# The opening of a four-layer decoder trunk: the input's two parts made straight from PSUM, its squares summed as loaded, and the first weights loaded in turns with the input

## The chip, the core and the metric

The kernel runs on one core of one Trainium2 chip. The metric is the device time of one execution in microseconds (us), lower is better. The core has a matrix engine (TensorE, PE in the rows; its weight loads are PEld), a vector engine (VectorE, DVE), an activation engine (ScalarE, ACT), GpSimd (POOL) and SyncE (SP), which here only issues transfers. The engines run side by side, each in the order of its own instructions, and wait for each other and for transfers at semaphores. TensorE writes only to PSUM, eight banks of 128 x 512 float32; the other tiles lie in SBUF.

## What is computed

The reference is a trunk of four layers on 256 tokens of width 1024. Each layer adds half a SwiGLU, a token mixer and another half SwiGLU to the residual stream, each behind an RMS norm:

```python
def swiglu(h, w_gate_up, w_down):
    g, u = jnp.split(h @ w_gate_up, 2, axis=-1)
    return (jax.nn.silu(g) * u) @ w_down
...
h = x
for layer in range(DEPTH):
    h = h + 0.5 * swiglu(rmsnorm(h, ffn_norm[layer, 0]), ffn_w_gate_up[layer, 0], ffn_w_down[layer, 0])
    h = h + mixer(rmsnorm(h, mixer_norm[layer]))
    h = h + 0.5 * swiglu(rmsnorm(h, ffn_norm[layer, 1]), ffn_w_gate_up[layer, 1], ffn_w_down[layer, 1])
```

The change touches only what happens before and during the first two pieces of the very first SwiGLU.

## The kernel before

All products are float32 products in three passes. Every operand is split into a high part, rounded to the matrix engine's fp32r format, and a low part, the remainder: `hi*hi + hi*lo + lo*hi`. So each weight block goes through ScalarE (`whi`, the rounded copy, `Weights.hi`, L126) and then VectorE (`wlo`, the difference, `Weights.lo`, L136). The input goes the same way: `xhi` by L294 and `xlo` by L303, both scaled by the norm's weights.

**Weights.** The class `Weights` streams all weights through four raw buffers of 128 x 2048 floats (`raw`), issued by SP in program order (L93). A raw buffer is cut into two *halves* of 128 x 1024, and each half becomes one `whi` and one `wlo`; there is room for six such halves. A *piece* of the first SwiGLU is 256 output columns (128 gate columns and 128 up columns) over all eight blocks of 128 input rows. It takes two halves: the first 128+128 columns of raw buffer 0 (input blocks 0 to 3) and those of raw buffer 1 (blocks 4 to 7). The second piece takes the other columns of the same two buffers. A piece is 8 blocks x 2 column halves x 3 passes = 48 products of 128x128 by 128x256.

**The opening.** `xin`, the input, comes in two transfers of 512 columns each (L255), then raw buffer 0 in four transfers of 128 columns (`L93`, 512-byte runs), then raw buffers 1, 2 and 3 in two transfers each with 1 KB runs. TensorE transposes `xin` into PSUM two blocks at a time (L2048, four transposes for two blocks, 16 in all), VectorE copies the result to `x` (L2050), ScalarE makes `xhi` from `x`, VectorE `xlo`, and GpSimd squares `x` (L2052). The squares are added on VectorE (L308), summed over the rows by four small products (`norm_sums`, L315), and turned into the norm's factor `rb` (`norm_rows`: L327, L329, L332), which scales the products afterwards. The products therefore need `xhi` and `xlo` but not the sum.

**Idle products.** `busy(n)` issues n products of constants (L272) that nothing reads, in places where TensorE would stand still.

**Order.** Everything is written out by hand; an engine's order is the order of the calls. The first piece is `first_cols` (blocks 0 to 3; L423 `whi` with `xhi` and `xlo` in turn, L427 `wlo`) and `late_cols` (blocks 4 to 7, L448: `whi` and `wlo` with `xhi` in turn, then `whi` with `xlo`). The second is `two_cols` (L335 to L337), with `norm_sums` before its block 2 and `norm_rows` before its block 5. Every later piece is `two_cols`; after each piece a `tail` (L486 to L502) makes the SwiGLU's hidden values from PSUM while the products of the next ones run.

## Time and profile before

| | |
|---|---|
| time of three runs | 2145.30, 2145.71, 2146.26 us; median 2145.71 |
| the profiled execution | time 2145.67 us, span 2143.9 us from the first to the last instruction |
| busy of the span | PE 99%, PEld 97%, DVE 66%, ACT 50%, POOL 13% |
| mean granted TensorE clock | 0.997 of full speed |

TensorE is busy in almost the whole span. Its busy time is the sum of modelled ends, so it is not the same as running at its peak; but a stretch in which it is not busy, or in which its clock is at half, is time that nothing later gives back as long as it is busy all the time behind it. The time that is not part of the span (1.8 us) lies around it.

### The profile page before, as it was taken

Reading aid. Unit: us, or ns where it says so; the run is one execution under the profiler, and the core shown is the slowest. Engines: PE = TensorE matmul, PEld = TensorE weight load, DVE = VectorE, ACT = ScalarE, POOL = GpSimd, SP = SyncE. Lnnn points to the kernel's source line nnn. Section 1 sums busy time; section 2 is a strip of 40 time slices with the busy share of each in tenths; the row PEclk is TensorE's granted clock in tenths of the full one; section 3 lists DMA queues with packets and bytes.
Section 4 is the critical chain, followed back from the end, with each engine's and each line's share of the span. In section 5 each row is a group of like instructions: output and inputs, shape, how many; then the busy total and the mean of one; then the engine's idle time right before and its main releaser. Section 6 shows DMA issues by size and latency. Waiting matters only on the chain. (4 is left out here: it accounts for less than half of the span.)

```text
span 2143.9 us, 42323 instructions
## 1 busy us (share of the span) xinstructions
PE 2120.5 (99%) x17599; PEld 2078.6 (97%) x17599; DVE 1408.4 (66%) x2326; ACT 1065.7 (50%) x1800; POOL 283.8 (13%) x312
## 2 busy tenths in 40 slices
PE   8999999999999999999999998999999999999999
PEld 8999999999999999999999987899999999999999
DVE  7664897665566476664666468866556648986653
ACT  5453754544454355444455445654445536655442
POOL 2210101121022010210121010012002101011110
PEclk9999999999999999999999999999999999999999
DMA  8564451556465555655566453155546563524652
GB/s 245 183 243 138 140 180 40 179 177 213 155 201 192 183 170 184 196 184 192 165 200 230 148 163 118 57 181 191 188 152 200 197 235 97 160 85 139 196 198 78
DMA packets 264304, 363.25 MB, mean 169 GB/s; under 512 B 17856, under 2 KB 212544, under 8 KB 264112
## 3 DMA queue, kind: packets, MB, share of 16 engines
q1 hardware_dynamic: 258320, 357.63, 50.8%
q8 instruction: 138, 2.26, 0.4%
q10 hardware_dynamic: 4848, 1.59, 0.4%
q0 software_dynamic: 944, 1.33, 0.3%
q14 instruction: 54, 0.44, 0.1%
HBM read 357.89 MB, written 2.10 MB: 168 GB/s over the span
## 5 line engine op out<-in xcount | busy, mean ns | idle before, releaser
L136 DVE TENSOR_TENSOR wlo<-raw,whi 128x1024 fp32r<-128x1024 f32 x640 | 775.2, 1219 | 234.8 <-ACT whi L126 234.4
L335 PE MATMUL acc<-xhi,whi 128*128 128x256 f32 x3248 | 911.4, 281 | 0.0
L337 PE MATMUL acc<-xhi,wlo 128*128 128x256 f32 x3248 | 909.4, 280 | 0.0
L336 PE MATMUL acc<-xlo,whi 128*128 128x256 f32 x3248 | 907.6, 279 | 0.0
L126 ACT ACTIVATE whi<-raw 128x1024 fp32r<-128x1024 f32 x633 | 660.2, 1050 | 352.5 <-PE mid L336 230.3
L336 PEld LDWEIGHTS acc<-xlo,whi 128*128 128x128 f32 x3248 | 611.1, 188 | 0.5
L337 PEld LDWEIGHTS acc<-xhi,wlo 128*128 128x128 f32 x3248 | 609.6, 188 | 0.0
L335 PEld LDWEIGHTS acc<-xhi,whi 128*128 128x128 f32 x3248 | 608.7, 187 | 0.5
L337 PE MATMUL mid<-hhi,wlo 128*128 128x256 f32 x1232 | 344.4, 280 | 0.0
L335 PE MATMUL mid<-hhi,whi 128*128 128x256 f32 x1232 | 343.7, 279 | 0.0
L336 PE MATMUL mid<-hlo,whi 128*128 128x256 f32 x1232 | 343.6, 279 | 0.0
L493 POOL TENSOR_TENSOR t_h<-t_gate,rb 128x256 f32<-128x256 f32 x176 | 197.8, 1124 | 738.9 <-ACT t_gate L489 731.3
L336 PEld LDWEIGHTS mid<-hlo,whi 128*128 128x128 f32 x1232 | 231.8, 188 | 0.0
L337 PEld LDWEIGHTS mid<-hhi,wlo 128*128 128x128 f32 x1232 | 231.2, 188 | 0.0
L335 PEld LDWEIGHTS mid<-hhi,whi 128*128 128x128 f32 x1232 | 230.9, 187 | 0.0
L489 ACT ACTIVATE t_gate<-t_gate 128x256 f32<-128x256 f32 x176 | 73.6, 418 | 311.0 <-DVE t_gate L488 311.0
L488 DVE TENSOR_TENSOR t_gate<-acc,rb 128x256 f32<-128x256 f32 x176 | 74.4, 422 | 187.5 <-PE acc L337 187.3
L495 DVE TENSOR_TENSOR t_h<-acc,t_h 128x256 f32<-128x256 f32 x176 | 74.7, 424 | 128.9 <-POOL t_h L493 128.9
L500 ACT ACTIVATE hhi<-t_h 128x256 fp32r<-128x256 f32 x176 | 73.7, 419 | 152.3 <-DVE t_h L495 152.3
L321 POOL TENSOR_TENSOR rcol<-rcol,neghalf 128x2 f32<-128x2 f32 x12 | 8.4, 704 | 654.6 <-DVE rcol L319 654.6
L502 DVE TENSOR_TENSOR hlo<-t_h,hhi 128x256 fp32r<-128x256 f32 x176 | 73.8, 420 | 7.8 <-ACT hhi L500 7.8
L294 ACT ACTIVATE xhi<-x,norms 128x256 fp32r<-128x256 f32 x96 | 43.3, 499 | 48.5 <-DVE x L379 42.2
(431 smaller groups left out, 2439.1 us busy)
## 6 DMA issues: line engine op xcount, KB each, us to landing
raw<-in_ffn_w_gate_up_dram SPq DMA_DIRECT2D x350, 512.0 KB, 5.3
raw<-in_ffn_w_down_dram SPq DMA_DIRECT2D x88, 1024.0 KB, 4.9
raw<-in_gdn_w_in_dram SPq DMA_DIRECT2D x32, 1024.0 KB, 5.3
raw<-in_nsa_w_in_dram SPq DMA_DIRECT2D x10, 1024.0 KB, 5.1
raw<-in_gdn_w_out_dram SPq DMA_DIRECT2D x8, 1024.0 KB, 5.2
raw<-in_sc_w_in_dram SPq DMA_DIRECT2D x16, 512.0 KB, 4.7
raw<-in_sc_w_in_dram SPq DMA_DIRECT2D x4, 1024.0 KB, 5.5
raw<-in_sc_w_out_dram SPq DMA_DIRECT2D x4, 1024.0 KB, 5.5
```

What stands on the lines that cost most here:

```text
L126: self.nc.scalar.activation(self.parts[g][0], raw, AF.Copy)
L136: (engine or self.nc.vector).tensor_sub(self.parts[g][1], self.half(g), self.parts[g][0])
L294: nc.scalar.activation(n.hi[:, kk], x[:, kk], AF.Copy, scale=norms[:, col + kk:col + kk + 1])
L335: nc.tensor.matmul(o, w[0], x[0], start=first, stop=False, skip_group_check=True)
L336: nc.tensor.matmul(o, w[0], x[1], start=False, stop=False, skip_group_check=True)
L337: nc.tensor.matmul(o, w[1], x[0], start=False, stop=last, skip_group_check=True)
L488: nc.vector.tensor_mul(t, acc[:, 0], n.rb)
L489: nc.scalar.activation(s, t, AF.Silu)
L493: nc.gpsimd.tensor_mul(sr, s, n.rb)
L495: nc.vector.tensor_mul(h, acc[:, 1], sr)
L500: nc.scalar.activation(hi, h, AF.Copy)
L502: nc.vector.tensor_sub(lo, h, hi)
```

## The change

The change has six parts, all in the opening.

1. `Weights.first` issues the first transfers: the input's first half, the first columns of raw buffer 0, the input's second half, the first columns of raw buffer 1, and then the other columns of both. Raw buffer 1 is now also loaded in four transfers of 512-byte runs.
2. `xhi` (now L2070) and `xlo` (L2076) are made from the transposes in PSUM; the copy to `x` is put off (`copies`, L2105, four on ScalarE during the second piece), since `x` is needed again only at the end of the SwiGLU.
3. The squares are taken on ScalarE from `xin` as it was loaded (L2081, with the row sum as a second output), so that there are no squares on GpSimd, no additions (L308) and no small products (L315) here; a VectorE addition of two sums remains (L338). `norm_rows` now stands before block 6 of the second piece.
4. The first `whi` is made on VectorE (`W.hi("V")`, L140), before the first `xlo`.
5. `first_cols` now does both halves of the first piece, and pass by pass: eight products of `whi` with `xhi`, eight with `xlo`, eight of `wlo` with `xhi` (L443).
6. The idle products write to other PSUM banks.

Behind the first two pieces each engine has the same instructions in the same order as before.

```diff
@@ -81,16 +81,28 @@
         names = "abc"[:len(dims)]
         return t[:, :n].rearrange(f"p ({' '.join(names)}) -> p {' '.join(names)}", **dict(zip(names, dims)))
+    def first(self, inputs):
+        srcs = self.srcs[:2]
+        raw = [self.view(self.raw_pool.tile([128, 2048], F32, name="raw"), x.shape[1:]) for x in srcs]
+        n = srcs[0].shape[3] // 2
+        for c in range(2):
+            for x in range(2):
+                if c == 0:
+                    self.nc.sync.dma_start(*inputs[x])
+                for b in range(2):
+                    self.nc.sync.dma_start(raw[x][:, :, b, c * n:c * n + n], srcs[x][:, :, b, c * n:c * n + n])
+        self.raw.update(enumerate(raw))
+        self.loaded = 2
+        self.load()
     def load(self):
         while not self.hold and self.loaded < min(self.freed + self.LOADS, len(self.srcs)):
             src = self.srcs[self.loaded]
             raw = self.view(self.raw_pool.tile([128, 2048], F32, name="raw"), src.shape[1:])
             if len(src.shape) == 4:
-                n = src.shape[3] // (1 if self.loaded else 2)
-                for c in range(0, src.shape[3], n):
-                    for b in range(src.shape[2]):
-                        self.nc.sync.dma_start(raw[:, :, b, c:c + n], src[:, :, b, c:c + n])
+                for b in range(src.shape[2]):
+                    self.nc.sync.dma_start(raw[:, :, b], src[:, :, b])
             else:
                 self.nc.sync.dma_start(raw, src)
             self.raw[self.loaded] = raw
@@ -251,9 +263,8 @@
     norm_rows = t2("norm_rows", (128,))[:96]
     nc.sync.dma_start(norm_rows[:64], a["ffn_norm"].rearrange("l i (k p) -> (l i k) p", p=128))
     nc.scalar.dma_start(norm_rows[64:], a["mixer_norm"].rearrange("l (k p) -> (l k) p", p=128))
-    for c in range(0, D, 512):
-        nc.sync.dma_start(xin[:, :, c:c + 512], a["x"][0, :, c:c + 512].rearrange("(t p) d -> p t d", p=128))
-    W.load()
+    W.first([(xin[:, :, c:c + 512], a["x"][0, :, c:c + 512].rearrange("(t p) d -> p t d", p=128))
+             for c in range(0, D, 512)])
     ij = const.tile([128, 128], I32, name="ij")
...
@@ -309,14 +323,20 @@
     def norm_sums(n):
-        p = bank()
-        for t in range(2):
-            for k in range(2):
-                nc.tensor.matmul(p[:, t:t + 1], n.sq[:, k, t * 128:(t + 1) * 128], ones[:, :1], start=k == 0,
-                                 stop=k == 1)
         n.r = work.tile([128, 2], F32, name="rcol")
+        if n.sums is None:
+            p = bank()
+            for t in range(2):
+                for k in range(2):
+                    nc.tensor.matmul(p[:, t:t + 1], n.sq[:, k, t * 128:(t + 1) * 128], ones[:, :1], start=k == 0,
+                                     stop=k == 1)
+            sums = p[:, :2]
+        else:
+            sums = n.r
         yield
-        nc.vector.tensor_scalar(n.r, p[:, :2], 1.0 / D, EPS, op0=OP.mult, op1=OP.add)
+        if n.sums:
+            nc.vector.tensor_add(n.r, *n.sums)
+        nc.vector.tensor_scalar(n.r, sums, 1.0 / D, EPS, op0=OP.mult, op1=OP.add)
         yield
         nc.gpsimd.tensor_tensor(n.r, n.r, neghalf[:, :2], op=OP.pow)
@@ -417,14 +437,11 @@
     def first_cols(j, acc, ks, n):
         parts = [[v.rearrange("p (s c) -> p s c", s=2) if len(v.shape) == 2 else v for v in W.part(j, k)] for k in ks]
-        for k, (hi, lo) in zip(ks, parts):
-            for s in range(2):
-                for x in (n.hi, n.lo):
-                    nc.tensor.matmul(acc[:, s], hi[:, s], x[:, k], start=k == 0 and s == 0 and x is n.hi, stop=False,
-                                     skip_group_check=True)
-        for k, (hi, lo) in zip(ks, parts):
-            for s in range(2):
-                nc.tensor.matmul(acc[:, s], lo[:, s], n.hi[:, k], start=False, stop=False, skip_group_check=True)
+        for w, x in ((0, n.hi), (0, n.lo), (1, n.hi)):
+            for k, both in zip(ks, parts):
+                for s in range(2):
+                    nc.tensor.matmul(acc[:, s], both[w][:, s], x[:, k], start=k == 0 and s == 0 and not w and x is n.hi,
+                                     stop=w == 1 and k == KT - 1, skip_group_check=True)
     def two_cols(j, acc, ks, n):
...
@@ -466,10 +481,13 @@
         W.use(pieces[1])
         for k in range(KT):
             if k == 2:
-                rest(norm_sums(n))
+                if n.sums is None:
+                    rest(norm_sums(n))
                 W.hi()
                 W.hi()
-            if k == 5:
+                if n.sums:
+                    n.copies()
+            if k == (5 if n.sums is None else 6):
                 norm_rows(n)
                 W.ahead(pieces[0] + 3)
             two_cols(pieces[1], accs[1], [k], n)
@@ -2037,33 +2055,57 @@
     for kind, layer, i in plan:
         cols.append((layer * 2 + i) * 8 if kind == "ffn" else 64 + layer * 8)
     cols.append(None)
-    n = norm_start()
-    busy(4)
-    for k in range(0, KT, 2):
-        if k == 4:
-            busy(4)
-        p = bank().rearrange("p (k t) -> p k t", k=2)
+    n = norm_start(False)
+    n.sums = [work.tile([128, 2], F32, name=f"xsum{h}", bufs=1) for h in range(2)]
+    def turned(k):
+        p = mid().rearrange("p (k t) -> p k t", k=2)
         for kk in range(2):
             for t in range(2):
                 nc.tensor.transpose(p[:, kk, t * 128:(t + 1) * 128],
                                     xin[:, t, (k + kk) * 128:(k + kk + 1) * 128], ident)
-        nc.vector.tensor_copy(x[:, k:k + 2], p)
-        norm_hi(n, k, cols[0], False)
-        nc.gpsimd.tensor_mul(n.sq[:, k:k + 2], x[:, k:k + 2], x[:, k:k + 2])
-        if k == 2:
-            W.hi()
-        if k:
-            norm_lo(n, k - 2, cols[0])
-        if k == 6:
-            W.lo()
-    norm_lo(n, KT - 2, cols[0])
-    W.ahead(0)
+        for kk in range(2):
+            c = cols[0] + k + kk
+            nc.scalar.activation(n.hi[:, k + kk], p[:, kk], AF.Copy, scale=norms[:, c:c + 1])
+        return p
+    def remains(k):
+        for kk in range(2):
+            c = cols[0] + k + kk
+            nc.vector.scalar_tensor_tensor(n.lo[:, k + kk], ps[k][:, kk], norms[:, c:c + 1], n.hi[:, k + kk],
+                                           op0=OP.mult, op1=OP.subtract)
+    def square_sums(h):
+        for t in range(2):
+            nc.scalar.activation(t2("xsq"), xin[:, t, 512 * h:512 * h + 512].rearrange("p (k c) -> p k c", k=2),
+                                 AF.Square, accum_out=n.sums[h][:, t:t + 1])
+    busy(4, "acc")
+    ps = {k: turned(k) for k in (0, 2)}
+    W.hi("V")
+    remains(0)
+    remains(2)
+    W.lo()
+    square_sums(0)
+    W.hi()
+    busy(4, "acc")
+    for k in (4, 6):
+        ps[k] = turned(k)
+        remains(k)
+    W.lo()
     W.hi()
     W.hi()
-    W.lo()
-    for k in range(2, KT, 2):
-        norm_squares(n, k)
+    square_sums(1)
     W.ahead(1)
+    rest(norm_sums(n))
+    def copies():
+        for k in ps:
+            nc.scalar.activation(x[:, k:k + 2], ps[k], AF.Copy)
+    n.copies = copies
     def loads_of(kind, i):
         return gdn_loads(g, i) if kind == "gdn" else nsa_loads(g, i) if kind == "nsa" else iter(())
```

The first place is SP's order of issue. `raw_81` and `raw_79` are raw buffer 0 before and now, `raw_86` and `raw_80` raw buffer 1; the waits are for the semaphores of earlier transfers. Before:

```order
L252 DMA norm_rows_76<-in_ffn_norm_dram 64x128
L255 DMA xin_75<-in_x_dram 128x2x512 x2
L93 DMA raw_81<-in_ffn_w_gate_up_dram 128x4x128 x4
L93 DMA raw_86<-in_ffn_w_gate_up_dram 128x4x256 [waits DMAHW0_49]
L93 DMA raw_86<-in_ffn_w_gate_up_dram 128x4x256 [waits DMAHW1_49]
L93 DMA raw_89<-in_ffn_w_gate_up_dram 128x4x256 [waits DMAHW2_49]
L93 DMA raw_89<-in_ffn_w_gate_up_dram 128x4x256 [waits DMAHW3_49]
L93 DMA raw_92<-in_ffn_w_gate_up_dram 128x4x256 [waits DMAHW4_49]
L93 DMA raw_92<-in_ffn_w_gate_up_dram 128x4x256 [waits DMAHW5_49]
```

Now:

```order
L264 DMA norm_rows_76<-in_ffn_norm_dram 64x128
L92 DMA xin_75<-in_x_dram 128x2x512
L94 DMA raw_79<-in_ffn_w_gate_up_dram 128x4x128 x2
L92 DMA xin_75<-in_x_dram 128x2x512
L94 DMA raw_80<-in_ffn_w_gate_up_dram 128x4x128 x2
L94 DMA raw_79<-in_ffn_w_gate_up_dram 128x4x128 [waits DMAHW0_49]
L94 DMA raw_79<-in_ffn_w_gate_up_dram 128x4x128 [waits DMAHW1_49]
L94 DMA raw_80<-in_ffn_w_gate_up_dram 128x4x128 [waits DMAHW2_49]
L94 DMA raw_80<-in_ffn_w_gate_up_dram 128x4x128 [waits DMAHW3_49]
L105 DMA raw_91<-in_ffn_w_gate_up_dram 128x4x256 [waits DMAHW4_49]
L105 DMA raw_91<-in_ffn_w_gate_up_dram 128x4x256 [waits DMAHW5_49]
L105 DMA raw_94<-in_ffn_w_gate_up_dram 128x4x256 [waits DMAHW6_49]
```

The input's second half moved behind raw buffer 0's first columns, and raw buffer 1's first columns moved ahead of raw buffer 0's second ones.

The second place is ScalarE's order between the first `xhi` and the weights of the second piece. The names with `whi` are, before, the halves 0 (`whi_143`), 1 (`whi_178`), 2 and 3. Before:

```order
L126 ACTIVATE whi_143<-raw_81 128x1024 [waits DMAHW5_49,DMAHW4_49]
L294 ACTIVATE xhi_117<-x_103,norms_112 128x256 [waits DVE_49]
L294 ACTIVATE xhi_117<-x_103,norms_112 128x256
L294 ACTIVATE xhi_117<-x_103,norms_112 128x256 [waits DVE_49]
L294 ACTIVATE xhi_117<-x_103,norms_112 128x256
L126 ACTIVATE whi_178<-raw_86 128x1024 [waits DMAHW1_49,DMAHW0_49]
L126 ACTIVATE whi_182<-raw_81 128x1024 [waits DMAHW7_49,DMAHW6_49]
L126 ACTIVATE whi_185<-raw_86 128x1024
```

Now, from the last `xhi` of blocks 0 to 3 (`mid` is a PSUM bank) and with half 1 as `whi_154`, half 2 as `whi_181`, half 3 as `whi_184`:

```order
L2070 ACTIVATE xhi_119<-mid_135,norms_114 128x256
L2081 ACTIVATE xsq_150,xsum0_121<-xin_75 128x512 [waits DMAHW2_49]
L2081 ACTIVATE xsq_152,xsum0_121<-xin_75 128x512
L138 ACTIVATE whi_154<-raw_80 128x1024 [waits DMAHW7_49,DMAHW6_49]
L2070 ACTIVATE xhi_119<-mid_162,norms_114 128x256 [waits PE_49]
L2070 ACTIVATE xhi_119<-mid_162,norms_114 128x256
L2070 ACTIVATE xhi_119<-mid_171,norms_114 128x256 [waits PE_49]
L2070 ACTIVATE xhi_119<-mid_171,norms_114 128x256
L138 ACTIVATE whi_181<-raw_79 128x1024 [waits DMAHW1_49,DMAHW0_49]
L138 ACTIVATE whi_184<-raw_80 128x1024 [waits DMAHW3_49,DMAHW2_49]
```

Half 0 is gone from ScalarE, two squares came in, and half 1 moved ahead of the `xhi` of blocks 4 to 7, which stand behind its wait for raw buffer 1.

The third place is VectorE's order in the first piece. Before (`wlo_144` is half 0, `wlo_179` half 1, `wlo_183` half 2):

```order
L2050 COPY x_103<-acc_134 128x512 [waits PE_49]
L303 SCALAR_TENSOR_TENSOR xlo_118<-x_103,norms_112,xhi_117 128x256 [waits Activation_49] x2
L2050 COPY x_103<-acc_153 128x512 [waits PE_49]
L303 SCALAR_TENSOR_TENSOR xlo_118<-x_103,norms_112,xhi_117 128x256 [waits Activation_49] x2
L2050 COPY x_103<-acc_164 128x512 [waits PE_49]
L303 SCALAR_TENSOR_TENSOR xlo_118<-x_103,norms_112,xhi_117 128x256 [waits Activation_49] x2
L136 TENSOR_TENSOR wlo_144<-raw_81,whi_143 128x1024 [waits DMAHW5_49,DMAHW4_49]
L303 SCALAR_TENSOR_TENSOR xlo_118<-x_103,norms_112,xhi_117 128x256 [waits Activation_49] x2
L136 TENSOR_TENSOR wlo_179<-raw_86,whi_178 128x1024 [waits DMAHW1_49,DMAHW0_49,Activation_49]
L136 TENSOR_TENSOR wlo_183<-raw_81,whi_182 128x1024 [waits DMAHW7_49,DMAHW6_49,Activation_49]
```

Now (`whi_142` and `wlo_143` are half 0, `wlo_155` half 1, `wlo_182` half 2):

```order
L140 CAST whi_142<-raw_79 128x1024 [waits DMAHW4_49,DMAHW3_49]
L2076 SCALAR_TENSOR_TENSOR xlo_120<-mid_128,norms_114,xhi_119 128x256 [waits DVE_49,PE_49,Activation_49]
L2076 SCALAR_TENSOR_TENSOR xlo_120<-mid_128,norms_114,xhi_119 128x256
L2076 SCALAR_TENSOR_TENSOR xlo_120<-mid_135,norms_114,xhi_119 128x256 [waits PE_49,Activation_49]
L2076 SCALAR_TENSOR_TENSOR xlo_120<-mid_135,norms_114,xhi_119 128x256
L148 TENSOR_TENSOR wlo_143<-raw_79,whi_142 128x1024 [waits DVE_49]
L2076 SCALAR_TENSOR_TENSOR xlo_120<-mid_162,norms_114,xhi_119 128x256 [waits PE_49,Activation_49]
L2076 SCALAR_TENSOR_TENSOR xlo_120<-mid_162,norms_114,xhi_119 128x256
L2076 SCALAR_TENSOR_TENSOR xlo_120<-mid_171,norms_114,xhi_119 128x256 [waits PE_49,Activation_49]
L2076 SCALAR_TENSOR_TENSOR xlo_120<-mid_171,norms_114,xhi_119 128x256
L148 TENSOR_TENSOR wlo_155<-raw_80,whi_154 128x1024 [waits DMAHW7_49,DMAHW6_49]
L148 TENSOR_TENSOR wlo_182<-raw_79,whi_181 128x1024 [waits DMAHW1_49,DMAHW0_49,Activation_49]
```

The copies and the additions of squares are gone, a rounded copy came in at the head, half 0's `wlo` moved ahead of the `xlo` of blocks 4 to 7, and half 1's `wlo` stands behind all eight `xlo`.

## Rows read from the trace of the kernel before

**Rows 1.** Busy time by stretch: us, PE, PEld, DVE, ACT, POOL, PE clock, DMA share, GB/s.

```profile
7.77:10.17 2.40, 0.88 (x9) 0.64 (x6) 2.40 (x4) 2.21 (x4) 1.71 (x2) 1.00 1.20 297
12.61:15.30 2.69, 0.00 (x2) 0.01 (x1) 2.69 (x4) 2.33 (x4) 1.21 (x1) 1.00 1.10 349
16.00:19.36 3.36, 3.18 (x16) 2.88 (x15) 3.26 (x5) 1.85 (x2) 0.00 (x0) 0.50 0.89 281
27.98:140.00 112.02, 112.02 (x954) 112.02 (x953) 76.33 (x131) 57.21 (x84) 26.98 (x28) 1.00 0.61 199
```

**Rows 2.** Timeline of TensorE: start us, duration us, what; [idle before <- releaser].

```profile
5.79 1.10 PE L2048 MATMUL acc<-ident,xin 128*128 128x128 f32 x8
6.72 1.05 PE L272 MATMUL mid<-ident,ones 128*128 128x128 f32 x8
...
10.18 0.38 PE L423 MATMUL acc<-xhi,whi 128*128 128x256 f32 x1 [1.53 <-ACT whi L126]
...
15.30 1.53 PE L427 MATMUL acc<-xhi,wlo 128*128 128x256 f32 x8 [2.69 <-DVE wlo L136]
...
21.01 0.28 PE L335 MATMUL acc<-xhi,whi 128*128 128x256 f32 x1
...
22.42 0.95 PE L315 MATMUL acc<-ones,sq 128*128 128x1 f32 x8
...
27.98 0.28 PE L335 MATMUL acc<-xhi,whi 128*128 128x256 f32 x1
```

**Rows 3.** Timeline of ScalarE.

```profile
7.21 1.71 ACT L294 ACTIVATE xhi<-x,norms 128x256 fp32r<-128x256 f32 x4 [4.73 <-DVE x L2050]
9.06 1.06 ACT L126 ACTIVATE whi<-raw 128x1024 fp32r<-128x1024 f32 x1
...
13.84 4.07 ACT L126 ACTIVATE whi<-raw 128x1024 fp32r<-128x1024 f32 x4 [0.36 <-DMA raw<-in_ffn_w_gate_up_dram]
```

**Rows 4.** Timeline of VectorE.

```profile
12.46 1.65 DVE L303 SCALAR_TENSOR_TENSOR xlo<-x,norms,xhi 128x256 fp32r<-128x256 f32 x2
14.03 1.21 DVE L136 TENSOR_TENSOR wlo<-raw,whi 128x1024 fp32r<-128x1024 f32 x1
15.16 0.87 DVE L303 SCALAR_TENSOR_TENSOR xlo<-x,norms,xhi 128x256 fp32r<-128x256 f32 x2
15.96 2.34 DVE L136 TENSOR_TENSOR wlo<-raw,whi 128x1024 fp32r<-128x1024 f32 x2
...
23.40 0.16 DVE L319 TENSOR_SCALAR rcol<-acc 128x2 f32<-128x2 f32 x1 [1.76 <-PE acc L315]
...
24.37 0.48 DVE L327 TENSOR_SCALAR dg<-ident,rcol 128x128 f32<-128x128 f32 x2 [0.81 <-POOL rcol L321]
```

**Rows 5.** The input's two transfers, by tile: first and last issue, time to landing.

```profile
L255 SPq DMA_DIRECT2D xin<-in_x_dram x2: 469/516/562, 1.4 to 2.0; - x2
...
DMA to landing us min/median/max: 4.4/4.8/5.2
```

**Rows 6.** Raw buffer 0's four transfers of 256 KB, by tile.

```profile
L93 SPq DMA_DIRECT2D raw<-in_ffn_w_gate_up_dram x4: 470/663/833, 2.5 to 4.4; - x4
...
DMA to landing us min/median/max: 5.6/6.1/6.3
```

**Rows 7.** Groups by line and form over the whole span, ScalarE.

```profile
L299 ACT ACTIVATE sq<-x 128x512 f32<-128x512 f32 x44 | 27.4, 623 | 8.9 <-DVE x L379 8.9
...
L1889 ACT ACTIVATION_READ_ACCUMULATOR np<-mid,nnm 128x1 f32 x64 | 12.8, 200 | 0.0
...
L1726 ACT ACTIVATE kv<-acc,rcol 128x256 f32<-128x256 f32 x4 | 1.9, 482 | 0.0
```

**Rows 8.** The same, VectorE.

```profile
L488 DVE TENSOR_TENSOR t_gate<-acc,rb 128x256 f32<-128x256 f32 x176 | 74.4, 422 | 187.5 <-PE acc L337 187.3
...
L128 DVE CAST whi<-raw 128x1024 fp32r<-128x1024 f32 x7 | 4.8, 686 | 0.0
```

More of the change, by code (lines that the diff above doesn't have):

```diff
@@ L266, with busy @@
     nc.vector.memset(neghalf, -0.5)
-    def busy(times):
-        p = mid()
+    def busy(times, tag="mid"):
+        p = bank(tag)
         for _ in range(times):
@@ L282, with norm_start @@
     class Normed:
-        pass
-    def norm_start():
+        sums = None
+    def norm_start(squares=True):
         n = Normed()
         n.hi, n.lo = b8(F32R, "xhi"), b8(F32R, "xlo")
-        n.sq = b8(F32, "sq")
+        if squares:
+            n.sq = b8(F32, "sq")
         return n
@@ L454, in dense @@
         W.use(j)
-        if j == 0:
-            first_cols(j, acc, range(4), n)
-        else:
-            (late_cols if first else two_cols)(j, acc, range(4), n)
-        (late_cols if first else two_cols)(j, acc, range(4, KT), n)
+        f = first_cols if j == 0 else late_cols if first else two_cols
+        f(j, acc, range(4), n)
+        f(j, acc, range(4, KT), n)
         W.retire(j)
```

## The prediction

> **What bounds the kernel now.** I read the busy times by stretch first. From 27.98 us, where the third piece's products begin, to 140 us TensorE is busy without a break at full clock, 954 products in 112.02 us, 0.1174 us each [rows 1]; over the whole span it is busy 99%. So behind the opening TensorE sets the pace, and there each engine has the instructions it had. What the change can win or lose is how much sooner or later the third piece's first product starts. Then TensorE's timeline: the first product starts at 10.18, the second piece's first at 21.01, the third piece's first at 27.98 [rows 2]. At 0.1174 the first piece's 48 products take 5.64 us; they took 10.83. The 5.2 us lost are, by stretch: no product from 12.61 to 15.30, and from 16.00 to 19.36 the granted clock at half (1.2 GHz of 2.4), 16 products in 3.36 us where 1.88 would do, 1.5 lost [rows 1]; the rest is short waits. The 2.69 us wait ends with half 0's `wlo` [rows 2]. That stood on VectorE from 14.03 to 15.24, behind the `xlo` of blocks 4 and 5 from 12.46, which took 1.65 for two where two others took 0.87 [rows 4] (GpSimd's squares run in that time), and half 1's rounded copy waited for its transfer until 13.84 [rows 3].
>
> **The loads now.** The input's first half lands at 1.4 + 4.4 = 5.8 and the second at 2.0 + 5.2 = 7.2, 1.4 apart [rows 5]. Raw buffer 0's four transfers land from 2.5 + 5.6 = 8.1 to 4.4 + 6.3 = 10.7, 0.87 apart [rows 6]. The last is issued 6.3 before it lands, so the transfers are issued far ahead, and I take them one behind the other in the order of issue. Now: input 5.8, raw 0 first columns 7.55, input's second half 8.95, raw 1 first columns 10.7, second columns 12.45 and 14.2. Then buffers 2 and 3, at 349 GB/s [rows 1] 1.5 for 512 KB, at 17.2 and 20.2. The waits on SP for earlier semaphores cost nothing: each is for the transfer eight places earlier, which has landed well before the queue runs dry. Bounds: 0.75 for 256 KB at 349 GB/s, 0.87 as read; raw 1's first columns land between 10.2 and 10.7.
>
> **The first piece now, step by step.**
> - TensorE starts the second eight transposes at 9.0. Eight took 0.93 (5.79 to 6.72) [rows 2], so the first product starts at 9.95 instead of 10.18: the products stand behind the transposes in TensorE's order.
> - VectorE's rounded copy of half 0 takes 0.69 [rows 8], from 7.6 to 8.3. The four `xlo` of blocks 0 to 3 follow 0.40 apart (0.87 for two), done at 10.0, half 0's `wlo` at 11.1 (1.21) [rows 4]. PSUM as a source was not seen for this instruction; a VectorE operation of that shape from PSUM takes 0.42 [rows 8], a ScalarE one 0.48 [rows 7], and the `xhi` from SBUF came at 1.71 for four [rows 3]. I change nothing for it, and take 0.2 either way.
> - So 24 products run without a wait, to 9.95 + 2.82 = 12.77.
> - ScalarE: four `xhi` by 8.6 at the latest, two squares with their sums 2 x (0.62 + 0.20) [rows 7], done at 10.25. They lie in its wait for raw 1. The table load, which now waits for the norm's weights, ends before the transposes do. Half 1's rounded copy runs from 10.8 to 11.85 (1.06), the four `xhi` behind it end at 13.55 (1.71) [rows 3].
> - The next eight products need these `xhi` one by one, and end at 13.85 instead of 13.71.
> - VectorE's last two `xlo` wait for 13.55 and end at 14.45. Half 1's `wlo` follows, to 15.6. The eight products with `xlo` are done at 14.8; the last eight wait 0.85 us and end at 15.65 + 0.94 = 16.6.
>
> The second piece's first product therefore comes at 16.6 instead of 21.0: **4.4 us**.
>
> **The second piece.** L315 goes. Its eight matrix instructions lie between 22.42 and the next product, 0.95 busy [rows 2], of which the last runs on under its successor: 0.83 to 0.95, I take **0.9**. From 21.01 to 27.98 are 6.97 us; less 5.64 and 0.9 that leaves 0.43 for L329, which stays. The third piece starts at 16.6 + 5.64 + 0.43 = 22.7 instead of 27.98.
>
> **What is costed at nothing, with its cover.** Half 2's `wlo` ends at 16.75, just when the third product wants it (16.8); each 0.1 more costs 0.1. Half 3's ends at 17.9, wanted at 19.4. The second two squares end on ScalarE at 17.2. The factor's chain took 1.45 from L319 to the end of L327 (23.40 to 24.85) [rows 4]; with the added sum it ends at 19.5, wanted by L329 at 20.8. Buffer 3 lands at 20.2, its `wlo` is done at 23, wanted at 25.5. The four copies to `x` take 0.62 each (the shape of L299) [rows 7] on ScalarE from 21.4 to 23.9, in front of two rounded copies which the fourth piece wants only at 28.4. GpSimd's squares and VectorE's copies and additions go; they were off the path but in VectorE's way, and that gain is in the times above.
>
> **Sum.** 4.4 + 0.9 = 5.3 us from the profiled execution's 2145.67 (span 2143.9), which is 0.04 under the median: **2140.4**. The bounds of loads and PSUM, and whether VectorE's `xlo` of blocks 4 and 5 wait for one `xhi` or two (0.4), give 2139.4 to 2141.2 for this case.
>
> **Rivals.**
> - *The clock falls again.* In the kernel before, from 7.77 to 10.17 TensorE had only eight transposes and idle time, and the granted clock stayed 1.00; it was at half after 2.69 us without a product [rows 1]. Now the longest stretch without a product is 7.77 to 9.95, 2.2 us, a little shorter, and then 0.85 at 14.8. So I expect no fall. The price, 3.36 us at half from 9.95: 16 products by 13.3, the eight `wlo` products of half 1 end at 17.05, 0.45 late, since the waits take up the rest; around the second gap up to 1.5. Time 2140.9 to 2141.9, chance 0.12.
> - *The turns don't bring half 1 forward.* If loads of 512-byte runs cost more side by side than in a row, or the queue keeps another order, raw 1's first columns land no sooner than the buffer did, 13.84. Then everything from half 1's copy on is 3.0 later: second piece at 19.65, a gain of 2.25, 2143.4. Chance 0.08. Against it: the four 256 KB loads landed in the order of issue.
> - *Slower than before.* The four `xhi` of blocks 4 to 7 now stand behind half 1's copy on ScalarE, and VectorE and TensorE behind them. Past 10.7 each microsecond of that transfer costs one: the gain of 5.3 is gone at a landing of 16.0, and it is 0.2% slower at 20.3. For it: nothing could overtake the wait. Against it: only 2.1 MB stand before that transfer, and before the change the same 2.1 MB had landed at 10.7 [rows 6]. Priced at a landing of 20.3: 2150. Chance 0.03. The Trainium skill (DMA: Bandwidth & Descriptors, sections Anatomy of one DMA and Bandwidth) advises against cutting loads small: it fits 2.0 us plus bytes at 436 GB/s to one transfer (on GpSimd's path, not SP's) and wants 1 MiB in each. If each transfer here paid that in turn, my estimate from that page is 2.6 for 256 KB and 3.2 for 512 KB, a landing at 19.4 and a time of 2149. By that rule the change loses; the trace, with 0.87 from landing to landing, doesn't agree with it for transfers that are queued one behind the other, and I go by the trace.
> - *VectorE reaches the first tail late.* It has less lead over TensorE than before, since the second piece's products now run without losses and ScalarE has the copies in front. If the PSUM banks of the first piece come free too late, the fifth piece waits; up to 1 us, 2141.4. I count some 2 us of cover. Chance 0.05.
> - *More overlap than I count* (earlier loads, and the waits at 13.7 and 14.8 gone): the first piece without any loss from 9.95 gives 15.6 and 2139.4. Below that: chance 0.06.
>
> **Numbers.** The forecast has 0.66; it is the likeliest, so 2140.4. A measurement of this kernel tells about 0.2% (4.3 us) from no change, the line is 2141.4. Faster by more: the forecast nearly whole, half of the clock case, the last case and part of the tails, 0.76; within 0.2%: the turns and the other halves, 0.21; slower 0.03. The range 2139.2 to 2143.0 leaves out the turns, the slower case and part of the last, under 0.2.
>
> **What would show it.** Right: first L443 at about 9.95; half 1's copy on ScalarE starting at about 10.8 as the transfer's wait ends; the last eight L443 starting at about 15.6 behind a VectorE wait of under 1 us; L355 at 16.6; the third piece at 22.7; granted clock 1.00 through 30 us; no gap behind. Wrong: half 1's copy starting past 12, `xlo` or `xhi` from PSUM above 0.5, the clock at half anywhere, or TensorE waiting behind 23 us.

## The result: 1.3% slower, by a cause that is nowhere in the diff's instructions

The changed kernel takes 2173.83 us (median, 2172.78 to 2174.7), the kernel before 2145.99 beside it: ratio 1.0128, 95% interval 1.0116 to 1.014. Forecast were 2140.4 and a gain of 5.3; measured is a loss of 27.8.

The opening did gain. TensorE's timeline of the changed kernel, from the second transposes to the third piece's first product (columns as in [rows 2]; L2066 are now the transposes, L443 the first piece, L355 to L357 `two_cols`):

```profile
9.86 1.09 PE L2066 MATMUL mid<-ident,xin 128*128 128x128 f32 x8 [1.89 <-DMA xin<-in_x_dram]
10.71 1.20 PE L443 MATMUL acc<-xhi,whi 128*128 128x256 f32 x8
...
16.39 1.21 PE L443 MATMUL acc<-xhi,wlo 128*128 128x256 f32 x8 [0.63 <-DVE wlo L148]
17.44 0.28 PE L355 MATMUL acc<-xhi,whi 128*128 128x256 f32 x1
...
21.75 0.59 PE L349 MATMUL acc<-dg,ones 128*128 128x256 f32 x2
...
23.61 0.28 PE L355 MATMUL acc<-xhi,whi 128*128 128x256 f32 x1
```

The second piece starts at 17.44 instead of 21.01, the third at 23.61 instead of 27.98 [rows 2]: 4.37 us won. ScalarE, half 1's rounded copy and the `xhi` behind it:

```profile
11.72 1.06 ACT L138 ACTIVATE whi<-raw 128x1024 fp32r<-128x1024 f32 x1 [2.25 <-DMA raw<-in_ffn_w_gate_up_dram]
12.68 1.55 ACT L2070 ACTIVATE xhi<-mid,norms 128x256 fp32r<-128x256 f32 x4
```

So 32 us were lost behind the opening. The busy times by stretch (columns as in [rows 1]) show how:

```profile
27.98:140.00 112.02, 112.02 (x936) 112.02 (x936) 74.95 (x131) 57.31 (x86) 26.86 (x28) 1.00 0.63 203
400.00:600.00 200.00, 200.00 (x1668) 199.95 (x1667) 115.66 (x160) 92.81 (x131) 28.24 (x26) 1.00 0.55 180
```

TensorE is busy without a break and its granted clock is 1.00, as before, but in the 112.02 us where it had done 954 products it does 936. Of the kernel before, the second of these stretches:

```profile
400.00:600.00 200.00, 200.00 (x1699) 199.95 (x1699) 119.43 (x165) 96.05 (x134) 28.98 (x26) 1.00 0.57 186
```

200 / 1668 is 0.1199, 200 / 1699 is 0.1177: each product takes 2.2 ns more of TensorE's time. This time from one product's start to the next is called the pitch below. The matrix instructions and weight loads (PEld), grouped by form over the whole span (busy us, mean ns of one; these lengths are longer than the pitch, since each product runs on under its successor), after:

```profile
L355 PE MATMUL acc<-xhi,whi 128*128 128x256 f32 x3248 | 922.9, 284 | 0.0
L355 PE MATMUL mid<-hhi,whi 128*128 128x256 f32 x1232 | 348.8, 283 | 0.0
L355 PE MATMUL mid<-hhi,wboth 128*128 128x256 f32 x176 | 49.8, 283 | 0.0
L355 PEld LDWEIGHTS acc<-xhi,whi 128*128 128x128 f32 x3248 | 623.3, 192 | 0.5
```

and the same four of the kernel before:

```profile
L335 PE MATMUL acc<-xhi,whi 128*128 128x256 f32 x3248 | 911.4, 281 | 0.0
L335 PE MATMUL mid<-hhi,whi 128*128 128x256 f32 x1232 | 343.7, 279 | 0.0
L335 PE MATMUL mid<-hhi,wboth 128*128 128x256 f32 x176 | 49.8, 283 | 0.0
L335 PEld LDWEIGHTS acc<-xhi,whi 128*128 128x128 f32 x3248 | 608.7, 187 | 0.5
```

The products with `whi` and `wlo` grew from 279 or 281 ns to 283 or 284, their weight loads from 187 to 192. Those whose weights lie in a lent buffer (`wboth`) had 283 before and still do. The groups like these, three passes each with those of the mixers, count some 14,690 products; at 2.2 ns that is 32 us.

The third row of both holds the hint: the same instruction, on the same engine at the same clock, at two speeds, told apart only by where its weights lie. The change allocates two tiles of 128 x 2 floats for the sums (`xsum0`, `xsum1`), 32 bytes per partition each in the allocator's layout, ahead of the weights in SBUF. That moves the weights by 64 bytes:

```
                    x and hidden parts start   weights' parts start   distance modulo 256
kernel before       29408 + 8192 n             179616 + 4096 n        192
changed kernel      29408 + 8192 n             179680 + 4096 n          0
lent buffers        29408 + 8192 n             29408 + 8192 n           0
```

(These are the allocator's bytes within a partition, not the trace's.) My theory became that the distance between the tile a product streams and its weights sets its pace. The rival: something in the order that the change shifted by a place, such as the ring of ten `b8` buffers, of which the change takes one fewer, the PSUM banks, or the semaphores of the transfers.

### The profile page after: what moved, and what is told of

Its sections match the earlier page's. It is cut to its first block, busy times and chain, and to the rows that moved or that the text cites. A ratio compares the mean times of both kernels' runs of the same rounds, so it can differ in the third digit from the quotient of the medians.

```text
span 2171.9 us, 42311 instructions
## 1 busy us (share of the span) xinstructions
PE 2149.6 (99%) x17591; PEld 2110.2 (97%) x17591; DVE 1402.8 (65%) x2321; ACT 1068.8 (49%) x1811; POOL 277.5 (13%) x308
## 5 line engine op out<-in xcount | busy, mean ns | idle before, releaser
L355 PE MATMUL acc<-xhi,whi 128*128 128x256 f32 x3248 | 922.9, 284 | 0.0
L356 PE MATMUL acc<-xlo,whi 128*128 128x256 f32 x3248 | 919.0, 283 | 0.0
L357 PE MATMUL acc<-xhi,wlo 128*128 128x256 f32 x3248 | 919.0, 283 | 0.0
L355 PEld LDWEIGHTS acc<-xhi,whi 128*128 128x128 f32 x3248 | 623.3, 192 | 0.5
L356 PEld LDWEIGHTS acc<-xlo,whi 128*128 128x128 f32 x3248 | 623.4, 192 | 0.5
L357 PEld LDWEIGHTS acc<-xhi,wlo 128*128 128x128 f32 x3248 | 623.3, 192 | 0.0
L355 PE MATMUL mid<-hhi,whi 128*128 128x256 f32 x1232 | 348.8, 283 | 0.0
L356 PE MATMUL mid<-hlo,whi 128*128 128x256 f32 x1232 | 348.7, 283 | 0.0
L357 PE MATMUL mid<-hhi,wlo 128*128 128x256 f32 x1232 | 348.6, 283 | 0.0
L357 PEld LDWEIGHTS mid<-hhi,wlo 128*128 128x128 f32 x1232 | 236.5, 192 | 0.0
L355 PEld LDWEIGHTS mid<-hhi,whi 128*128 128x128 f32 x1232 | 236.5, 192 | 0.0
L308 ACT ACTIVATE xhi<-x,norms 128x256 fp32r<-128x256 f32 x88 | 39.7, 498 | 42.9 <-DVE x L399 42.9
```

What stands on the lines that cost most here:

```text
L308: nc.scalar.activation(n.hi[:, kk], x[:, kk], AF.Copy, scale=norms[:, col + kk:col + kk + 1])
L355: nc.tensor.matmul(o, w[0], x[0], start=first, stop=False, skip_group_check=True)
L356: nc.tensor.matmul(o, w[0], x[1], start=False, stop=False, skip_group_check=True)
L357: nc.tensor.matmul(o, w[1], x[0], start=False, stop=last, skip_group_check=True)
```

## The experiments

**The two tiles alone, in the kernel before.**

```diff
     n = norm_start()
+    for h in range(2):
+        work.tile([128, 2], F32, name=f"xsum{h}", bufs=1)
```

> The kernel before, instruction for instruction, with the two small tiles of the sums allocated and never used, so that weights, loads and the tiles behind them start 64 bytes further on, where the changed kernel has them. Placement theory: products 120 ns apart from the first one on, mean weight load 192 ns instead of 188, time about 2146 + 32 = 2178. Rival, anything in the changed order of instructions, buffers, banks or semaphores: the time stays at 2146.

2178.3 us, ratio 1.015 (1.0135 to 1.0165). Two tiles that nothing reads or writes cost 32 us. Against this run, at equal places, the changed kernel is 4.5 us quicker: that is what its instructions are worth.

**The changed kernel with the distance set back.** An unused tile behind the two, here of 192 bytes (the other sizes follow):

```diff
     n.sums = [work.tile([128, 2], F32, name=f"xsum{h}", bufs=1) for h in range(2)]
+    work.tile([128, 48], F32, name="gap", bufs=1)
```

> The changed kernel with 192 unused bytes behind the two small tiles. The distance from a streamed tile to the weights' parts is then 192 modulo 256, as in the kernel before (there 150208 bytes, here 150464; modulo 512 they differ, 192 and 448). Placement theory, place counted modulo 256: pitch 117.5 ns as before, time 2173.8 - 14,690 x 0.0022 to 0.0025 = 2137 to 2141.5, a ratio of 0.996 to 0.998, which is what the change itself is worth at an equal pitch. Counted modulo 512 or more: another pitch, no number. If the change lost something of its own behind the opening: over 2143.

2140.65 us, ratio 0.9974 (0.9965 to 0.9984): with the distance of before, the forecast's 2140.4 comes out. The addresses differ from those of before by 256 bytes, the ring, banks and semaphores are the changed kernel's. That rules out the rival of order.

**Other distances.**

> The changed kernel with 64 unused bytes per partition put behind the two small tiles of the sums, so that the weights' parts start at 179744 (32 bytes past a multiple of 128, as before) instead of 179680 (96 past one); the tiles that the products stream (x and hidden parts) stay at 96 past one. Placement theory: the 2.2 ns that each of some 14,690 products gained after the change come from where the two operands lie to each other, so the products behind the opening go back to 117.5 to 118 ns apart, the span falls by about 32 us to about 2139.5, the time to 2141 to 2142, and what is left against before is the opening's 4 to 4.5 us. Rival, the order of the buffers, PSUM banks or DMA semaphores that the change shifted by a place: none of that is touched here, so the products stay 120 ns apart and the time at 2174.

2088.36 us, ratio 0.9731 (0.9717 to 0.9746): not the 2141 that I expected. My figure took places 128 bytes apart to be alike, and they aren't. This is by far the quickest version, faster than both kernels by 58 and 85 us:

```profile
400.00:600.00 200.00, 200.00 (x1760) 199.77 (x1760) 124.83 (x171) 100.14 (x138) 29.89 (x28) 1.00 0.60 198
```

113.6 ns a product, with the clock at 1.00 and TensorE still busy throughout. The products whose weights lie in a lent buffer, at distance 0 in every run, keep their 283 ns here, where the same ones with `whi` fell from 283 to 277.

> The changed kernel with 32 unused bytes: weights' parts start on a multiple of 128, the streamed tiles 96 past one. Placement by the distance of the two modulo 128: the distance is 32 here, between the slow 0 and the quick 64; if only an equal place costs, 2141.5; if what counts is whether both lie in the same half of 128 bytes or of 64, it may stay at 2174. Placement by the weights' own start alone (bad at 96, good at 32): no number, 2141 or 2174. The rival of order: 2174.

> 96 unused bytes: distance 96 modulo 256. By the fall of 3.2 ns for each 32 bytes: 110 to 113.6 ns, time 2040 to 2088. If 64 is a best place with a rise on both sides: about 117 ns, 2145.

> 128 unused bytes: distance 128 modulo 256, as far from 0 as it goes. The pitches so far: 120.0 ns at 0, 117.0 at 32, 113.6 at 64, 117.5 at 192. If the cost falls with the distance from 0 (modulo 256) on either side, this is the lowest: at most 113.6, by the step of 3.2 ns for 32 bytes some 107 to 110, time 2020 to 2088. If the pattern repeats each 128 bytes with 64 the best: 120 ns and 2173, but then before's 192 should have been like 64, which it wasn't.

> 160 unused bytes: distance 160 modulo 256, between 128 and the 192 of before (117.5 ns). If the cost falls evenly up to 128 on either side: about 113 ns, 2085. If only the side from 0 to 128 gains, since the streamed tile is read from its start on while the weights are, 117 to 120 ns, 2140 to 2174.

> The changed kernel with 224 unused bytes: distance 224 modulo 256, the one that is missing. No theory gives its number; products alone had 117.8 there, which would make 2140 to 2144.

Products from 400 to 600 us of each profile, with the time (one execution each for 96, 160 and 224, medians else), and for comparison the pitch in the kernel of products in threes that is told below:

```
distance  products  ns each (200 us / products)  time us    in threes alone
   0        1668       119.9                      2173.83      120.0
  32        1691       118.3                      2149.78      118.3
  64        1760       113.6                      2088.36      113.3
  96        1687       118.6                      2149.6       118.6
 128        1686       118.6                      2155.74      118.6
 160        1668       119.9                      2173.79      120.0
 192        1699       117.7                      2140.65      117.8
 224        1715       116.6                      2129.24      116.7
```

My guess of an even fall from 0 to 128 was wrong: 64 stands alone, and 160 is as slow as 0. The 117.0 ns at 32 that the expectations go by is 118.3 in this stretch, and 224 is quicker than the 2140 to 2144 expected from the products alone.

**Is it the distance, or where the weights start? Is it the weights, or the raw buffers?** Everything moved by 32 bytes (a tile ahead of all others), the same with 64 more behind the sums, and 64 bytes between raw buffers and parts only.

> The changed kernel with 32 unused bytes ahead of everything that it allocates: the streamed tiles and the weights' parts both start on a multiple of 128, so their distance is still 0. By the distance: products 120 ns apart, 2174. By the weights' own start (bad only at 96, or bad because it is no multiple of 64): 2141 to 2142, or lower. The rival of order: 2174, which does not tell it from the distance; the run with 64 bytes does.

> Streamed tiles on a multiple of 128 bytes and parts 64 bytes past one: both 32 bytes further than in the run with 64 unused bytes, the distance the same, 64 modulo 256. By the distance alone: pitch 113.5 ns, 2088. By the parts' own start (179776, where the run with 96 unused bytes has them too): pitch 117 to 118 and 2150, as there.

> The changed kernel with 64 unused bytes between the raw buffers and the weights' parts: only the parts move (to 179744, as with 64 bytes behind the two small tiles), while the raw buffers and the small tiles stay where the changed kernel has them. If the distance between the two operands of a product is what counts: pitch 113.5 ns, 2088. Rival, that the raw buffers' place counts (ScalarE and VectorE read them, transfers write them, all through the run): pitch 120, 2174.

2171.37 (ratio 1.0118, 1.0103 to 1.0133), 2088.12 and 2087.91 (one execution each). With parts at 179712 a product takes 119.9 ns here (1668 in the stretch) and 118.3 with the streamed tiles 32 bytes lower (`after_gap32`); with parts at 179776 it is 113.6 here and 118.6 in `after_gap96`. So the weights' start alone does not decide, and the raw buffers' place doesn't matter. Moving both operands together (`after_all32`) leaves the pitch where it was.

**The kernel before at the quickest distance.**

> The kernel before, with the two small tiles and 64 unused bytes allocated and not used: the distance is 64 modulo 256, as in the changed kernel with 64 unused bytes (2088.36). If the change is worth the same 4.5 to 5.2 us as at the distances 0 (2178.3 to 2173.8) and 192 (2145.8 to 2140.65): 2093 to 2093.6. If the lower pitch makes other engines the bound in the opening or the change's gain depends on it: outside 2091 to 2095.

2094.65, ratio 0.976 (0.9744 to 0.9777). The change gains 6.3 here, 5.15 at 192 and 4.5 at 0: a little more than the range that I gave, and in no case a loss.

**Products alone.** The core of the kernel:

```python
def run(name, n, dx, dw, cols=256):
    p = psum.tile([128, 512], F32, name=name, tag="p", bufs=8)
    for i in range(n):
        xo, wo = dx(i) // 4 + 256 * (i % 4), dw(i) // 4 + 128 * (i % 8)
        nc.tensor.matmul(p[:, :cols], w[:, wo:wo + 128], x[:, xo:xo + cols], start=True, stop=True, ...)
for d in range(0, 512, 32):
    run(f"d{d}", 96, lambda i: 0, lambda i: d)
```

> This kernel leaves out the whole trunk: it copies the input to the output and issues only float32r products of 128x128 by 128x256 (96 for each setting, some of 128x512) that nothing reads, with no other engine at work. Groups d0 to d480: weights so many bytes past the streamed tile, modulo 512. If the operands' distance alone sets the pitch: 120 ns at 0, 117 at 32, 113.5 at 64, 118 at 96 and 128, 119.5 at 160, 117.5 at 192, and d256 to d480 repeat d0 to d224. If other engines' reads are needed: one pitch for all, about 107 to 113. Groups own0_nextS: the distance within each product is 0, that from its stream to the next product's weights is S; groups ownS_next0 the other way round. If the next product's weight load meets the present stream: own0_next64 at 113.5 like d64, all of ownS_next0 at 120 like d0. If a product's own load meets its own stream: own0_next64 at 120 and own64_next0 at 113.5. In the wide groups (512 columns, 213 ns of streaming) the load has more room: by either theory smaller differences, a few ns.

Busy times by stretch; each reaches from the start of a group's 17th product to that of its 89th, so its length by 72 is the pitch. In turn distances 0, 64, 128, 192, 256 and 320, then `own0_next64`, `own64_next0` and `own0_next128`:

```profile
31.14:39.78 8.64, 8.64 (x75) 8.64 (x73) 0.00 (x0) 0.00 (x0) 1.00 0.01 2
53.98:62.46 8.48, 8.48 (x75) 8.48 (x73) 0.00 (x0) 0.00 (x0) 1.00 0.00 0
76.59:85.23 8.64, 8.64 (x74) 8.64 (x73) 0.00 (x0) 0.00 (x0) 1.00 0.01 2
99.59:108.07 8.48, 8.48 (x74) 8.48 (x73) 0.00 (x0) 0.00 (x0) 1.00 0.00 0
122.24:130.88 8.64, 8.64 (x75) 8.64 (x73) 0.00 (x0) 0.00 (x0) 1.00 0.01 2
145.08:153.56 8.48, 8.48 (x75) 8.48 (x73) 0.00 (x0) 0.00 (x0) 1.00 0.00 0
236.27:244.79 8.52, 8.52 (x75) 8.52 (x73) 0.00 (x0) 0.00 (x0) 1.00 0.00 0
315.83:324.35 8.52, 8.52 (x75) 8.52 (x73) 0.00 (x0) 0.00 (x0) 1.00 0.01 2
259.09:267.49 8.40, 8.40 (x75) 8.40 (x73) 0.00 (x0) 0.00 (x0) 1.00 0.01 2
```

120.0 at 0, 117.8 at 64, 120.0 at 128, 117.8 at 192, and 256 and 320 repeat 0 and 64. VectorE and GpSimd stand at 0.00 and ScalarE runs nothing, so no other engine is needed, and the pattern repeats each 256 bytes. Three things came out otherwise than expected. Distances 64 and 128 gave 117.8 and 120.0, not the trunk's 113.6 and 118.6. The question which read meets which has no simple answer: `own0_next64` and `own64_next0` both come to 118.3, between the theories, and `own0_next128` to 116.7. A weight load lasts some 188 ns and the products start 118 apart, so by the records each load runs beside the stream ahead of it and the start of its own.

The third is the wide groups. Here are 32 products of 512 columns each, from a group's 9th to its 41st, at distances 0 and 64:

```profile
383.91:391.17 7.26, 7.26 (x34) 6.01 (x33) 0.00 (x0) 0.00 (x0) 1.00 0.01 2
406.04:413.51 7.47, 7.47 (x33) 6.02 (x32) 0.00 (x0) 0.00 (x0) 1.00 0.00 0
```

That is 226.9 ns at 0, the quickest of the eight distances there, and 233.4 at 64: the differences are larger than with 256 columns, not smaller, and the order of the distances is another.

**Products in the trunk's order.** The same with `whi`, `wlo`, `xhi` and `xlo` as four tiles, in threes as `two_cols` has them, and each difference undone by itself.

> Leaves out the whole trunk as the first kernel of products did. Groups of 96 products in the trunk's own order (whi with xhi, whi with xlo, wlo with xhi, for two column halves of each block, summed up in two halves of a bank), at distances 0 to 240 in steps of 16 bytes; then at 0, 64, 128 and 192 with one thing undone each: no sums kept, one half of the bank, and single products instead of threes (plain, with both halves of the bank, with two tiles each). If the order of the reads makes the difference: threes at 113.5 for 64 and, as in the trunk, 120 at 0, 117 at 32, 118 at 96, 118.5 at 128, 119.5 at 160, 117.5 at 192, with or without sums or halves, and singles at 117.8 for 64 as in the first kernel of products. If PSUM makes it: no_sums or one_half at 117.8 for 64. If neither, so that only the trunk's surroundings give 113.5: all groups at 64 at 117.8.

Distances 0, 64 and 192 in threes, then at 64 without sums (each product overwrites PSUM instead of adding to it), in one half of the bank, and as single products with sums:

```profile
37.58:46.22 8.64, 8.64 (x74) 8.64 (x73) 0.00 (x0) 0.00 (x0) 1.00 0.00 0
83.02:91.18 8.16, 8.16 (x74) 8.16 (x73) 0.00 (x0) 0.00 (x0) 1.00 0.00 0
173.88:182.36 8.48, 8.48 (x74) 8.48 (x73) 0.00 (x0) 0.00 (x0) 1.00 0.00 0
230.62:239.10 8.48, 8.48 (x75) 8.48 (x73) 0.00 (x0) 0.00 (x0) 1.00 0.01 2
276.10:284.26 8.16, 8.16 (x75) 8.16 (x74) 0.00 (x0) 0.00 (x0) 1.00 0.01 2
321.21:329.37 8.16, 8.16 (x75) 8.16 (x73) 0.00 (x0) 0.00 (x0) 1.00 0.01 2
```

8.16 / 72 is 113.3 ns, the trunk's pace, and 8.48 / 72 the 117.8 of the first kernel of products: at 64 the sums alone make the difference here. The order of the reads, the halves of the bank and the number of tiles change nothing. At 0, 128 and 192 the sums make none either (120.0, 118.6 and 117.8 with and without). So the 120.0 that the first kernel had at 128 is not explained by its missing sums; what else differs between the two kernels of products was not separated. In steps of 16 bytes 64 stands alone too: 48 has 117.8, 80 has 118.8, and no other of the sixteen is under 116.7. The column "in threes alone" of the table above is this kernel's; it agrees with the trunk within 0.4 ns at all eight distances.

**The loads in turns, undone** (at the distance of before).

```diff
-        for c in range(2):
-            for x in range(2):
-                if c == 0:
-                    self.nc.sync.dma_start(*inputs[x])
-                for b in range(2):
-                    self.nc.sync.dma_start(raw[x][:, :, b, c * n:c * n + n], srcs[x][:, :, b, c * n:c * n + n])
+        for x in range(2):
+            self.nc.sync.dma_start(*inputs[x])
+        for c in range(2):
+            for b in range(2):
+                self.nc.sync.dma_start(raw[0][:, :, b, c * n:c * n + n], srcs[0][:, :, b, c * n:c * n + n])
+        for b in range(2):
+            self.nc.sync.dma_start(raw[1][:, :, b], srcs[1][:, :, b])
```

> The changed kernel at the distance of before (192 unused bytes, 2140.65), with the loads in the old order: both halves of the input, raw buffer 0 in four, raw buffer 1 in two. My recorded steps: half 1 is there when all of raw buffer 1 is, about 13.8 as before, instead of 11.3, so half 1's rounded copy, the four xhi, the xlo and the wlo behind it come 2.5 later, the second piece's first product at 19.5 instead of 17.05, time 2143.1. The input's second half lands earlier, so that the second transposes start at about 7.5 to 8. Rival: the turns are worth nothing, second piece at 17 and 2140.7.

2143.59 us, 2.9 over the 2140.65 with the turns (ratio to before 0.9989, 0.9979 to 0.9998). Half 1's rounded copy on ScalarE, TensorE, and then the busy times of three stretches:

```profile
14.18 1.06 ACT L139 ACTIVATE whi<-raw 128x1024 fp32r<-128x1024 f32 x1 [4.55 <-DMA raw<-in_ffn_w_gate_up_dram]
15.65 1.60 PE L444 MATMUL acc<-xhi,whi 128*128 128x256 f32 x8 [2.19 <-ACT xhi L2072]
17.09 1.81 PE L444 MATMUL acc<-xlo,whi 128*128 128x256 f32 x8
18.84 1.99 PE L444 MATMUL acc<-xhi,wlo 128*128 128x256 f32 x8
20.67 0.28 PE L356 MATMUL acc<-xhi,whi 128*128 128x256 f32 x1
```

```profile
13.46:15.65 2.19, 0.00 (x1) 0.00 (x0) 0.00 (x0) 1.47 (x3) 0.00 (x0) 1.00 1.10 348
17.50:20.00 2.50, 2.50 (x12) 2.26 (x12) 2.50 (x4) 2.50 (x7) 0.00 (x0) 0.50 0.59 186
15.65:20.67 5.02, 5.02 (x24) 4.57 (x25) 4.67 (x7) 5.02 (x11) 0.00 (x0) 0.66 0.70 221
```

The second piece comes at 20.67, not 19.5. Half 1's rounded copy starts at 14.18 here and at 11.34 with the turns, and the last eight products, which wait for its `wlo`, come the same 2.84 later (18.84 for 16.00). From there the second piece would start at 19.89, as it does 1.05 behind them with the turns. The other 0.78 is the clock: behind a wait of 2.19 us, the first stretch, it is at half (1.2 GHz of 2.4) from 17.5 to 20.0. So in the profiled executions the turns are worth 2.84 by the transfer's lead and 0.78 by the clock. The medians lie only 2.9 apart, so it is not shown that the clock falls in every execution.

**The parts from `x` in SBUF again** (at the distance of before): `turned` copies each pair of blocks to `x` on VectorE, `norm_hi` and `norm_lo` read it, the late copies go.

> The changed kernel at the distance of before (192 unused bytes), with the parts made from x in SBUF as before: VectorE copies each pair of blocks from PSUM (0.68 us each), ScalarE's xhi and VectorE's xlo read the copy, and the four late copies on ScalarE go. Blocks 0 to 3 are hidden by the second transposes. VectorE's copy of blocks 6 and 7 stands behind its xlo of 4 and 5, which wait for ScalarE: that copy from about 14.1, xlo of 6 and 7 to 16.4, half 1's wlo to 17.6 instead of 15.95. Second piece's first product at 18.4 to 18.6 instead of 17.05, time 2142.1. Rival: all of it is covered, 2140.7.

2141.61 us, 0.96 over 2140.65 (ratio to before 0.9981, 0.9971 to 0.999; the two intervals overlap, so the size is read from TensorE's timeline):

```profile
13.35 0.63 PE L443 MATMUL acc<-xhi,whi 128*128 128x256 f32 x4
15.11 0.91 PE L443 MATMUL acc<-xhi,whi 128*128 128x256 f32 x4 [1.13 <-ACT xhi L308]
...
18.18 0.28 PE L355 MATMUL acc<-xhi,whi 128*128 128x256 f32 x1
```

The second piece starts at 18.18 instead of 17.05: the `xhi` of blocks 6 and 7 wait for VectorE's copy, as expected, 0.2 to 0.4 us milder.

**One distance, two paces.** The distance does not settle the pace alone. The stretches below reach from the first of some products to the one behind their last: 36 of the second piece in `gap192_old_loads`, the same 36 in `after_gap192` (each operand at the same address in the allocator's layout), 72 with the hidden parts (`hhi`, `hlo`) at distance 192 in the kernel before, and 72 such at 64 in `after_gap64`:

```profile
20.67:24.76 4.09, 4.09 (x38) 4.09 (x37) 2.25 (x6) 4.09 (x8) 0.70 (x1) 1.00 0.78 235
17.05:21.29 4.24, 4.24 (x39) 4.24 (x37) 3.02 (x7) 1.60 (x4) 0.70 (x1) 1.00 1.10 350
177.33:185.49 8.16, 8.16 (x74) 8.16 (x73) 3.31 (x3) 3.19 (x3) 0.00 (x0) 1.00 0.39 144
165.11:173.59 8.48, 8.48 (x74) 8.48 (x73) 3.11 (x3) 2.12 (x2) 0.00 (x0) 1.00 0.62 229
```

4.09 / 36 is 113.6 ns and 4.24 / 36 is 117.8; then 113.3 stands at 192, where most products have 117.8, and 117.8 at 64, where most have 113.3. All of them add to PSUM. What ran just before differs: products at half clock before the first stretch, products with lent weights before the last two; and the other engines and the transfers do other work beside them. Which of these decides is not shown. Such stretches are few, so the times by distance hold.

## Why the prediction was wrong

**The step that failed** is "So behind the opening TensorE sets the pace, and there each engine has the instructions it had", with what follows from it: "What the change can win or lose is how much sooner or later the third piece's first product starts." The instructions were the same; their operands lay 64 bytes elsewhere, and I took 0.1174 us a product over from the kernel before as if it belonged to the instruction. At 2.2 ns for some 14,690 products the step is 32 us wide, six times the whole sum. No rival held it: the slower one was a late transfer in the opening, and all others stayed within 5 us as well. The two tiles alone bring the loss to the kernel before (2178.3), and the distance of before takes it from the changed kernel (2140.65). None of the prediction's signs of being wrong showed it: half 1's copy started at 11.72, `xhi` and `xlo` from PSUM took some 0.4 each, the clock stayed at 1.00 through the opening, and TensorE's waits behind 23 us were those of before within half a microsecond each. Each sign looked at the opening, at the clock or at a wait, and a longer pitch behind the opening is none of these.

**The opening, step by step**, is judged at the pace that the steps assumed, that is on `after_gap192`:

```profile
9.49 1.09 PE L2067 MATMUL mid<-ident,xin 128*128 128x128 f32 x8 [1.57 <-DMA xin<-in_x_dram]
10.34 1.19 PE L443 MATMUL acc<-xhi,whi 128*128 128x256 f32 x8
...
16.00 1.21 PE L443 MATMUL acc<-xhi,wlo 128*128 128x256 f32 x8 [0.63 <-DVE wlo L148]
17.05 0.28 PE L355 MATMUL acc<-xhi,whi 128*128 128x256 f32 x1
...
23.14 0.28 PE L355 MATMUL acc<-xhi,whi 128*128 128x256 f32 x1
```

Half 1's rounded copy on ScalarE there:

```profile
11.34 1.06 ACT L138 ACTIVATE whi<-raw 128x1024 fp32r<-128x1024 f32 x1 [1.93 <-DMA raw<-in_ffn_w_gate_up_dram]
```

- *Loads.* The order held, and the turns bring half 1 forward by 2.8 us (14.18 on ScalarE with the old loads, 11.34 here). The landings were priced some 0.5 us early: second transposes at 9.49 instead of 9.0, half 1's copy at 11.34 instead of 10.8 (11.72 in the changed kernel's own profile). The estimate from a price for each transfer in turn (the Trainium skill, DMA: Bandwidth & Descriptors, Anatomy of one DMA) put that transfer's landing at 19.4; the trace, with the copy behind it at 11.34, doesn't agree.
- *First piece.* First product 10.34 for 9.95, last eight at 16.00 behind a wait of 0.63 for 15.65 behind 0.85, second piece 17.05 for 16.6: the 0.5 of the loads, passed on.
- *PSUM as source.* `xhi` 1.55 for four (the changed kernel's second row on ScalarE above), against 1.71 from SBUF [rows 3]; `xlo` 1.66 for four, against 0.87 for two [rows 4]. So at most 0.16 won for either, within the 0.2 that was left open.
- *L315.* The second piece takes 6.09 (17.05 to 23.14) instead of 6.97: 0.88 for the 0.9.
- *Third piece* at 23.14 for 22.7: 4.84 won of 5.3, and 5.15 in the medians.
- *The clock* stayed at 1.00 as forecast; the changed kernel's longest wait in the opening is 1.89 us. With the old loads it was at half behind one of 2.19.

## What to carry to other kernels

A pitch that is read from a trace holds for the operands where they lay. Before a product's duration is carried over to a changed kernel, compare the bases of the streamed tiles and of the weights, since a tile of a few bytes that is allocated ahead of them can cost or win a per cent or more. Where TensorE is the bound, try unused gaps of 32 to 224 bytes between the two pools, anew for each form of product (with 512 columns distance 0 was the quickest), and compare two versions of a kernel only at equal distances. Count the products over a long stretch, since one distance can show two paces. In the profile, one instruction form at two durations that differ only in the pool of an operand is the sign to look for.

## What the runs showed of the hardware

- The pitch of most 128x128 by 128x256 float32r products in the trunk, and of the groups in one kernel of products, follows the distance from the streamed tile to the weights, modulo 256 bytes: 113.3 to 120.0 ns, at full granted clock, with no other engine at work. The Trainium skill (SBUF — State Buffer, Who interferes with whom) gives TensorE two independent read ports and names one shared port pair of other engines as the only place of contention. By that rule alone the groups would be alike; they are not, and the measurement decides. No run shows whether the difference arises at the ports.
- In the kernels of products, at a distance of 64, groups that add to PSUM run at 113.3 ns and groups that overwrite it at 117.8; at 0 and 192 both have one pitch. In the trunk, products that add to PSUM run at either pace, at 64 as at 192, a few per cent of them at the one that is not usual there.
- Why it is 256 bytes, why 64 is the quickest with 256 columns, why the sums matter there, and what chooses between two paces at one distance is not settled. That the two reads of TensorE get in each other's way was argued from the load's 188 ns, not shown: setting the distance within a product and that to the next product's weights apart gave 116.7 to 121.7 ns, by neither theory. Distances other than multiples of 32 bytes were tried in products alone, not in the trunk.
